# First mixer: convolution taps on VectorE, norms by fours, and the copies of queries and keys issued by GpSimd, head 0's before the value projections

## The chip, the cores and the metric

The kernel runs on one core of a Trainium2 chip. The metric is the device time of one execution in microseconds (us). Several executions are timed, and one more is recorded by the hardware profiler. All times below on a common axis ("at 487 us") count from the start of the span of that profiled execution. Engines are named as the profile names them: PE is TensorE's matmuls, PEld its weight loads, DVE is VectorE, ACT is ScalarE, POOL is GpSimd, SP is SyncE; "POOLq" and "SPq" are DMA issues on those engines' queues.

## The reference, cut to what matters

A sequence of 512 tokens of width 1024 passes through feed-forward blocks and mixers. The change touches one mixer, the first. It has two halves whose outputs are concatenated and projected: a gated delta net (4 heads of 128) and an attention (8 heads of 64) with a bias that depends on the distance of query and key.

```
qkv = silu(short_conv(qkv, conv_w))            # 5 taps along the tokens, per channel
q, k, v = l2_normalize(qkv[0]), l2_normalize(qkv[1]), qkv[2]
...                                            # decay g and beta per token and head
tmat = triangular_solve(eye + lmat, eye)       # chunks of 64 tokens
o    = scan over the chunks, forward and backward
o    = rms_norm(o_fwd + o_bwd, norm_w) * silu(z)
...
logits = q k^T + bias                          # the attention half
out = softmax(logits) v
```

Here l2_normalize divides by the root of the sum of squares over the 128 features of a head; the attention's queries and keys get an RMS norm of their own over 64 features.

## The kernel before, in words

Data in float32 is split into a high and a low part in a reduced format, and each product of two such matrices is three matmuls of TensorE (xh by wh, xh by wl, xl by wh). So each weight block is loaded by a DMA (`raw`, SyncE's queue), cast by ScalarE (`wh`) and subtracted by VectorE (`wl`) before TensorE can use it. The sequence of work on each engine is set by a scheduler from the code's order and the dependences; each engine runs its own queue in order, and buffers come from pools with a tag and a number of slots, which rotate.

The first mixer lasts from about 396 to 870 us. Its parts, in the order of the code:

- **Convolution.** Twelve tiles of 128 channels by 512 tokens (m = 0 to 3 queries, 4 to 7 keys, 8 to 11 values) go through a pipeline of three steps, `conv`, `sums`, `rest`, in which step j of tile m runs beside step 0 of tile m + j. `conv` projects a tile (`pqkv` in PSUM), scales it into a padded tile (`pad`, VectorE), and makes five taps: the first by ScalarE, the other four by VectorE (`cv<-pad,vc,cv`). For m = 8 and 9 the four taps are made by ScalarE into `tap` and added by GpSimd. Then comes a Silu (ScalarE). `sums` squares a query or key tile (`sq`, ScalarE), sums over the features with TensorE (`pss`), and makes the inverse root on VectorE, in `rsqrt`, a chain of 11 small ops with three Newton steps, and in all 14 small ops with the scaling ahead and the split into high and low behind (`rv`, `rt`, `ry`, `yh`, `yl`, 128x4 each). `rest` spreads the result over the features with TensorE (`pn`) and multiplies the tile. For a value tile `rest` turns it (TensorE, `pvt`; copied out by ScalarE, `vt`).
- **Decays.** Per head the products of keys with keys and queries (`pkk`, `pqk`) and the decays (`pgr`, `et`), from which the tiles `B` and `IT` come.
- **Solve.** A triangular solve of 32x32 blocks for all heads on VectorE, 31 steps of two ops (`dX`, `dT`), with a way out to memory and back (`dgi`, `dR`), and then two levels of products per head (`bl` made by GpSimd, `py` by TensorE).
- **Scan.** 32 units (`psc`, `pso`, `vn`); its operands come back from memory by GpSimd's queue (`ld<-ntd`).
- **Norm of O**, four tiles, one by one, each with its own `rsqrt`.
- **Attention.** Projections of queries and keys (`psw`) in pairs of tiles with a norm by pairs (`Ym`, `yxm`, 128x16), written to memory (`qkd`, GpSimd's queue). Value projections (`psv`). Then a pipeline over 8 heads by 4 query tiles: `prepare(h)` brings two copies of a head's keys and of its queries from memory (`T<-qkd`), casts them (ScalarE, `K`, `Q`), and takes the low parts (GpSimd); it also loads the bias (`bq`). `pS` are the scores, `P` the softmax exponentials (ScalarE), `ptp` and `PT` the turn, `po` the product with the values. `prepare(h + 1)` is called at the second query tile of head h, `prepare(0)` at the very first.
- **Gate.** `psz` are projections of the gate z, whose Silu needs another activation table on ScalarE than the exponential (`ACT_TABLE_LOAD`).

The code's order is not the engines' order: the matmuls of `psw`, `psv` and `psz` depend on little and are put between the steps of the convolution, the solve, the scan and the attention. After the attention GpSimd loads four tables for a later mixer (`uqt`) and copies parts of them (`uq`). The buffers of `T` come from the tag `sT` (5 slots), shared with `pad` and the projections' tiles; `sqt` (3 slots) is the tag of the squares.

Of the kernel before, what the change touches and what calls it, by code (L numbers as in the profile page):

```python
# [13 lines left out]
AF = mybir.ActivationFunctionType  # L14
ALU = mybir.AluOpType
# [3 lines left out]
NT = 512  # L19
# [185 lines left out]
class Builder:  # L205
# [424 lines left out]
        return dst  # L630


    def copies(self, src, s, n, tag):
# [6 lines left out]
    def stackK(self, src, s, tags, rows=True):  # L640

        T = self.copies(src, s, 2, tags[0])
# [7 lines left out]
    def stackQ(self, src, s, tags, rows=True):  # L650

        T = self.copies(src, s, 2, tags[0])
# [159 lines left out]
    def mixer1(self):  # L812
        nc = self.nc
        S, S0 = slice(MT, NC), slice(0, NT)
        toks = SEQ
        XH, XL, rs, rsc = self.norm(toks, "mix")
# [56 lines left out]
        def conv(m, _):  # L873
# [17 lines left out]

        def sums(m, cv):
            if m >= 8:
                self.act(cv, cv, AF.Silu)
            return cv, self.row_scales(cv, chunks, 128, 1.0, self.mx) if m < 8 else None

        def rest(m, got):
            cv, y = got
            if m < 8:
                self.row_apply(cv, y, chunks, 128, 128 ** -0.5 if m < 4 else 1.0, self.mx)  # L900
            else:
                pt = self.mx("pvt")
                for c in range(4):
                    self.tr(pt[:, 128 * c:128 * c + 128], cv[:, 128 * c:128 * c + 128])
                vt = self.slab("u", "vt", width=NT)
                self.acopy(vt, pt)
                cv = vt
            C[m] = cv

        staged(12, conv, sums, rest)  # L910
        q, k, vt = C[0:4], C[4:8], C[8:12]


# [169 lines left out]

        staged(32, old, values, update)

        for c in (1, 2, 0, 3):
            ss, sv, sy, sx = (self.small(n, 4, bufs=2) for n in ("nv4", "rv4", "ry4", "rt4"))
            sq = self.slab("u", "sq", width=NT)
            self.act(sq, O[c], AF.Square)
            nc.vector.tensor_reduce(out=ss, in_=by_c(sq), op=ALU.add, axis=mybir.AxisListType.X)  # L1090
            self.ts(sv, ss, 1.0 / 128, ALU.mult, EPS, ALU.add)
            self.rsqrt(sy, sv, sx)
            o3 = by_c(O[c])
            self.mul(o3, o3, sy.unsqueeze(2).to_broadcast([128, 4, 128]))


        sw = self.small("sw", 1)
# [15 lines left out]
        def normed(i, got):  # L1113
# [2 lines left out]
                nc.gpsimd.dma_start(out=qkd[m, :, S], in_=t[:, S])  # L1116

        staged(4, proj, sums, normed)
        V = [self.slab("V", "sV", width=NT) for _ in range(4)]
        staged(4, lambda m, _: self.projV(XH, XL, toks, "psv"), lambda m, t: self.turnV(  # L1120
            t, toks, lambda i, ps: self.act(V[i][:, cc[m]], ps, AF.Copy, scale=rsc[:, i:i + 1]), self.acc))


        Yh, Yl = [None] * 8, [None] * 8
# [2 lines left out]
        def prepare(h):  # L1127
            p, x = divmod(h, 2)
            r = slice(64 * x, 64 * x + 64)
            K = self.stackK(qkd[4 + p, r, :], S, ("sT", "u"), False)  # L1130
            Q = self.stackQ(qkd[p, r, :], S, ("sT", "u"), False)
            heads[h] = {"K": K, "Q": Q, "Y": heads[h - 1]["Y"] if x else self.slab("y", "Y", width=NT),
                        "bq": self.toeplitz(1, h, 0, 0, 896, bpool.tile([128, 1024], F32, tag="bq", name="bq", bufs=2)),
                        **{n: self.small("rs" + n, 4, bufs=2) for n in ("mx", "nm", "den", "rec")}}

        def scores(i, _):
            h, t = divmod(i, 4)
            if i == 0:
                prepare(0)
            if t == 1 and h < 7:  # L1140
                prepare(h + 1)
            u = heads[h]
# [702 lines left out]
```

## Time and profile before

| | us |
|---|---|
| median of 3 runs | 3268.3 (3267.72 to 3269.59) |
| the profiled execution's own time | 3267.1 |
| its span | 3265.3 |
| TensorE busy | 3136.8 |
| VectorE busy | 1747.0 |
| ScalarE busy | 1140.8 |
| GpSimd busy | 511.2 |

The span is the time from the first to the last instruction of the profiled execution; some 1.8 us lie around it. A row of a timeline gives the start, the duration, the engine, the line of the code (often a helper's), the operation, and what it writes and reads by the names above. In brackets stands how long the engine had been idle before it, and who released it.

### The profile page before, as it was taken

The page shows a single profiled execution, that of the slowest core. Times are in us where ns is not written, and L with a number is a line of the kernel's source. Part 1 is how long each engine was busy: PE and PEld are TensorE (multiplying, and loading weights), DVE is VectorE, ACT ScalarE, POOL GpSimd, SP SyncE. Part 2 cuts the span into 40 slices and gives each one's busy share as a digit, 9 for nine tenths or more (in the row PEclk, how much of TensorE's full clock was granted, in tenths as well). Part 3 has the DMA queues.
Part 4 walks back from the last instruction along what each step waited for, and adds up shares of the span by engine and source line. Part 5 has one row for each costly group of instructions (what it writes and reads, how often), then busy time and mean ns, then how long its engine had stood idle before and what let it go on. Part 6 is the DMA issues. An engine that isn't in the chain of part 4 may idle for free. (4 is left out here: it accounts for less than half of the span.)

```text
span 3265.3 us, 47205 instructions
## 1 busy us (share of the span) xinstructions
PE 3136.8 (96%) x18654; PEld 2678.6 (82%) x18654; DVE 1747.0 (54%) x3602; ACT 1140.8 (35%) x1946; POOL 511.2 (16%) x605
## 2 busy tenths in 40 slices
PE   8999989898999999998999999999999899999998
PEld 6778768876788889988887999999878686688886
DVE  4443377653444445764676744433675386754433
ACT  4322253256422233222554332222322364232221
POOL 1000010322000011432123400000351223400000
PEclk9999999898999999998999999999999899999999
DMA  4334313233223324233342523233223343523332
GB/s 132 100 98 132 98 59 97 83 106 94 71 92 96 94 94 125 81 93 106 120 125 86 180 91 91 91 95 119 87 83 116 124 137 100 183 91 96 92 95 79
DMA packets 121270, 337.24 MB, mean 103 GB/s; under 512 B 28853, under 2 KB 29248, under 8 KB 121048
## 3 DMA queue, kind: packets, MB, share of 16 engines
q1 hardware_dynamic: 87656, 267.95, 26.3%
q0 software_dynamic: 21712, 54.51, 5.5%
q10 hardware_dynamic: 11680, 11.76, 1.1%
q8 instruction: 147, 2.41, 0.3%
q14 instruction: 75, 0.61, 0.1%
HBM read 298.42 MB, written 39.56 MB: 104 GB/s over the span
## 5 line engine op out<-in xcount | busy, mean ns | idle before, releaser
L269 ACT CAST wh<-raw 128x1024 fp32r<-128x1024 f32 (+1 forms) x448 | 462.9, 1034 | 1465.8 <-issue 629.6
L247 DVE TENSOR_TENSOR wl<-raw,wh 128x1024 fp32r<-128x1024 f32 (+1 forms) x448 | 556.1, 1242 | 428.2 <-ACT wh L269 427.0
L241 PE MATMUL pg<-xl,wh 128*128 128x512 f32 (+1 forms) x880 | 282.2, 353 | 13.1 <-DVE xl L259 13.1
L241 PE MATMUL pg<-xh,wl 128*128 128x512 f32 (+1 forms) x880 | 280.5, 351 | 0.0
L241 PE MATMUL pg<-xh,wh 128*128 128x512 f32 (+1 forms) x880 | 280.4, 351 | 0.0
L241 PE MATMUL pu<-xl,wh 128*128 128x512 f32 (+1 forms) x880 | 280.2, 351 | 0.0
L241 PE MATMUL pu<-xh,wl 128*128 128x512 f32 (+1 forms) x880 | 280.0, 351 | 0.0
L241 PE MATMUL pd<-hl,wh 128*128 128x512 f32 (+1 forms) x880 | 279.8, 351 | 0.0
L241 PE MATMUL pd<-hh,wl 128*128 128x512 f32 (+1 forms) x880 | 279.3, 350 | 0.0
L241 PE MATMUL pu<-xh,wh 128*128 128x512 f32 (+1 forms) x880 | 279.2, 350 | 0.0
L241 PE MATMUL pd<-hh,wh 128*128 128x512 f32 (+1 forms) x880 | 278.6, 349 | 0.0
L241 PE MATMUL pgz<-xl,wh 128*128 128x264 f32 (+1 forms) x768 | 223.3, 339 | 8.3 <-ACT wh L269 6.8
L247 DVE TENSOR_TENSOR fb<-pu,rs 128x512 f32<-128x512 f32 (+1 forms) x110 | 62.7, 586 | 287.7 <-PE pu L241 287.7
L241 PE MATMUL pgz<-xh,wl 128*128 128x264 f32 (+1 forms) x768 | 214.1, 328 | 1.8 <-DVE wl L247 1.8
L241 PE MATMUL pgz<-xh,wh 128*128 128x264 f32 (+1 forms) x768 | 213.8, 329 | 0.0
L241 PEld LDWEIGHTS pg<-xl,wh 128*128 128x128 f32 x880 | 154.5, 189 | 38.4 <-DVE xl L259 15.2
L241 PEld LDWEIGHTS pu<-xh,wl 128*128 128x128 f32 x880 | 154.4, 189 | 25.1 <-issue 2.6
L241 PEld LDWEIGHTS pg<-xh,wl 128*128 128x128 f32 x880 | 155.0, 189 | 24.1 <-issue 1.7
L241 PEld LDWEIGHTS pg<-xh,wh 128*128 128x128 f32 x880 | 154.5, 189 | 24.4 <-issue 0.9
L241 PEld LDWEIGHTS pu<-xh,wh 128*128 128x128 f32 x880 | 153.9, 188 | 24.0 <-issue 0.9
L241 PEld LDWEIGHTS pd<-hh,wh 128*128 128x128 f32 x880 | 153.8, 188 | 23.5
L241 PEld LDWEIGHTS pd<-hh,wl 128*128 128x128 f32 x880 | 154.0, 188 | 22.6
(496 smaller groups left out, 6343.8 us busy)
## 6 DMA issues: line engine op xcount, KB each, us to landing
raw<-in_win SPq DMA_DIRECT2D x136, 512.0 KB
raw<-in_gu SPq DMA_DIRECT2D x88, 512.0 KB
raw<-in_f1gu SPq DMA_DIRECT2D x44, 512.0 KB
raw<-in_f2gu SPq DMA_DIRECT2D x44, 512.0 KB
raw<-in_dn SPq DMA_DIRECT2D x32, 512.0 KB
raw<-in_wout SPq DMA_DIRECT2D x24, 512.0 KB
gates<-g POOLq DMA_DIRECT2D x32, 264.0 KB, 2.8
gr<-gates SPq DMA_DIRECT2D x32, 264.0 KB
```

Source lines behind the costliest of these rows:

```text
L241: return self.nc.tensor.matmul(out=out, lhsT=lhsT, rhs=rhs, start=start, stop=stop)
L247: return (eng or self.nc.vector).tensor_tensor(out=out, in0=a, in1=b, op=op)
L269: return self.nc.scalar.copy(out=out, in_=in_)
```

## The change

- `conv`: for all tiles the taps two to five are made by VectorE, and the Silu follows in `conv`; `tap` and GpSimd's additions are gone.
- `sums` of the convolution: the four query tiles get one chain of small ops together (`group_scales`, on 128x16, in `Ym` and `yxm`), at m = 3, and the four key tiles at m = 7, instead of one chain on 128x4 per tile. They are multiplied in the third step, now `scaled`, two tiles each at m = 4, 5, 8 and 9.
- Norm of O: by twos, one chain on 128x8 for two tiles.
- `prepare(h)`: both copies `T<-qkd` are issued by GpSimd instead of SyncE, into the tag `sqt`; `prepare(0)` is called ahead of the value projections.

```diff
+    def copies(self, src, s, n, tag, eng=None):
...
-        self.nc.sync.dma_start(out=t[:n * rows, s], in_=src[:, s].unsqueeze(0).to_broadcast([n, rows, w]))
+        (eng or self.nc.sync).dma_start(out=t[:n * rows, s], in_=src[:, s].unsqueeze(0).to_broadcast([n, rows, w]))
...
             for i in range(1, 5):
-                if m not in (8, 9):
-                    self.stt(cv, pad[:, i:i + 512], self.v("conv", 5 * m + i), cv, ALU.mult, ALU.add)
-                else:
-                    t = self.slab("u", "tap", width=NT)
-                    self.act(t, pad[:, i:i + 512], AF.Copy, scale=self.v("conv", 5 * m + i))
-                    self.add(cv, cv, t, nc.gpsimd)
-            if m < 8:
-                self.act(cv, cv, AF.Silu)
+                self.stt(cv, pad[:, i:i + 512], self.v("conv", 5 * m + i), cv, ALU.mult, ALU.add)
+            self.act(cv, cv, AF.Silu)
             return cv
...
         def sums(m, cv):
+
+            C[m] = cv
+            if m in (3, 7):
+                ys.update(zip(range(m - 3, m + 1), self.group_scales(C[m - 3:m + 1], chunks, 128, 1.0, self.mx)))
+
+        def scaled(m, _):
+            for i in {4: (0, 1), 5: (2, 3), 8: (4, 5), 9: (6, 7)}.get(m, ()):
+                self.row_apply(C[i], ys[i], chunks, 128, 128 ** -0.5 if i < 4 else 1.0, self.mx)
             if m >= 8:
...
-        for c in (1, 2, 0, 3):
-            ss, sv, sy, sx = (self.small(n, 4, bufs=2) for n in ("nv4", "rv4", "ry4", "rt4"))
...
+        for two in ((1, 2), (0, 3)):
+            ss, sv, sy, sx = (self.small(n, 8, bufs=2) for n in ("nv8", "rv8", "ry8", "rt8"))
...
+            K = self.stackK(qkd[4 + p, r, :], S, ("sqt", "u"), False, nc.gpsimd)
+            Q = self.stackQ(qkd[p, r, :], S, ("sqt", "u"), False, nc.gpsimd)
...
+        prepare(0)
         V = [self.slab("V", "sV", width=NT) for _ in range(4)]
```

The instructions move on several engines, which the diff alone doesn't show. On VectorE, in the convolution, at the norms of the last key tiles, the order before has two chains of small ops interleaved (`rt_3145` and `rt_3223` are those of two tiles):

```order
L259 SCALAR_TENSOR_TENSOR rt_3145<-rt_3145,rv_3144 128x4
L263 TENSOR_SCALAR rv_3222<-pss 128x4
L259 SCALAR_TENSOR_TENSOR ry_3146<-rt_3145,ry_3146 128x4
L263 TENSOR_SCALAR rt_3223<-rv_3222 128x4
L247 TENSOR_TENSOR rt_3145<-ry_3146 128x4
L263 TENSOR_SCALAR ry_3224<-rt_3223 128x4
```

The order after, at the end of the chain of the four key tiles:

```order
L259 SCALAR_TENSOR_TENSOR Ym<-Ym 128x16 x2
L247 TENSOR_TENSOR wl<-raw,wh 128x1024
L272 CAST yxm<-Ym 128x16
L259 SCALAR_TENSOR_TENSOR cv<-pad,vc,cv 128x512
L247 TENSOR_TENSOR yxm<-Ym,yxm 128x16
L259 SCALAR_TENSOR_TENSOR cv<-pad,vc,cv 128x512 x3
L259 SCALAR_TENSOR_TENSOR cv<-cv,pn 128x512 x2
```

One chain for four tiles has taken the place of four; its end stands among the taps of a value tile, ahead of the multiplication of the key tiles (`cv<-cv,pn`). On GpSimd, at the start of the attention, behind the last loads of the scan, the order before is this (`K` and `Q` are the low parts; the numbers tell the heads apart, 5513 and 5518 are head 0's):

```order
L1044 DMA ld<-itd 128x512
L247 TENSOR_TENSOR K_5513<-T,K_5512 64x512
L247 TENSOR_TENSOR Q_5518<-T,Q_5518 64x512
L247 TENSOR_TENSOR K_5538<-T,K_5537 64x512
L247 TENSOR_TENSOR Q_5543<-T,Q_5543 64x512
L629 DMA bq<-bper_575 128x1x896
```

The order after (5167 and 5172 are head 0's):

```order
L1037 DMA ld<-itd 128x512
L629 DMA uqt<-bper_584 128x1x416
L247 TENSOR_TENSOR K_5167<-T,K_5166 64x512
L629 DMA uqt<-bper_584 128x1x416
L247 TENSOR_TENSOR Q_5172<-T,Q_5172 64x512
L637 DMA T<-qkd 128x1x512 x2
L1207 COPY uq<-uqt 128x64
L1209 COPY uq<-uqt 128x16
```

The loads `uqt` of the later mixer, which stood behind head 5 before, stand here by twos; the copies `uq` of the first two come next, and the key part of head 1 behind them, and the copies `T` of later heads stand between the parts; both copies of head 0 and the key copy of head 1 are not among these rows, since they are issued some 30 instructions earlier, beside the masks `bl`. On ScalarE, in the middle of the attention, the order before has other work between a gate's Silu and the second of its two table loads:

```order
L266 ACT_TABLE_LOAD
L266 ACTIVATE z<-z 128x512
L269 COPY yt<-ptr 128x512
L266 ACTIVATE Y<-po,rsrec 128x64
L269 CAST Yh<-yt 128x512
L269 COPY PT<-ptp 128x512
L266 ACT_TABLE_LOAD
L266 ACTIVATE P,rsden<-P,rsnm 128x512
```

In the order after it is like this there, and at each of the four gates:

```order
L269 CAST wh<-raw 128x1024
L269 COPY PT<-ptp 128x512
L266 ACTIVATE Y<-po,rsrec 128x64
L266 ACT_TABLE_LOAD
L266 ACTIVATE z<-z 128x512
L266 ACT_TABLE_LOAD
L266 ACTIVATE P,rsden<-P,rsnm 128x512 x2
```

The two loads of a pair have only the Silu between them now; before, this was so at two gates of four.

## Rows read from the trace of the kernel before

**Rows 1.** The page, busy time of TensorE: us, share of the span, instructions.

```profile
PE 3136.8 (96%) x18654; PEld 2678.6 (82%) x18654; DVE 1747.0 (54%) x3602; ACT 1140.8 (35%) x1946; POOL 511.2 (16%) x605
```

**Rows 2.** Timeline of TensorE in the convolution, and its first py.

```profile
480.74 0.40 PE L241 MATMUL pqkv<-xh,wh 128*128 128x512 f32 x1
487.37 0.45 PE L241 MATMUL pn<-idr,yl 128*128 128x128 f32 x1 [6.23 <-DVE rt L247]
...
507.83 0.39 PE L241 MATMUL psw<-xl,wh 128*128 128x512 f32 x1
508.06 0.40 PE L241 MATMUL psw<-xh,wl 128*128 128x512 f32 x1
...
508.90 0.39 PE L241 MATMUL pkk<-cv 128*128 128x128 f32 x2
...
604.02 1.13 PE L241 MATMUL py<-n,bl 128*128 128x128 f32 x8 [0.96 <-DVE n L247]
```

**Rows 3.** Windows: length, busy us by engine, granted clock, DMA share, GB/s.

```profile
490.00:500.00 10.00, 10.00 (x50) 8.66 (x50) 7.14 (x36) 0.63 (x1) 0.00 (x0) 0.78 0.18 52
720.00:730.00 10.00, 9.57 (x39) 7.73 (x39) 2.95 (x11) 7.16 (x14) 0.60 (x2) 0.67 0.28 87
780.00:790.00 10.00, 10.00 (x39) 8.06 (x38) 2.27 (x6) 5.84 (x13) 3.07 (x7) 0.50 0.43 129
790.00:800.00 10.00, 9.73 (x51) 7.69 (x49) 3.97 (x14) 4.58 (x11) 2.70 (x5) 0.76 0.38 102
800.00:810.00 10.00, 5.98 (x18) 4.06 (x19) 2.80 (x8) 3.02 (x8) 2.49 (x5) 0.58 0.17 51
```

**Rows 4.** Timeline of TensorE in the attention, the ends of three holes.

```profile
720.43 1.11 PE L244 MATMUL ptp<-ct,P 128*128 128x128 f32 x4 [4.02 <-ACT P L266]
...
779.41 0.48 PE L244 MATMUL ptp<-ct,P 128*128 128x128 f32 x1 [3.35 <-ACT PT L269]
...
804.02 1.51 PE L241 MATMUL pS<-K,Q 128*128 128x512 f32 x2 [4.29 <-POOL Q L247]
```

**Rows 5.** Timeline of VectorE: small ops of two norms, one whole chain's ends, the solve.

```profile
477.81 0.17 DVE L263 TENSOR_SCALAR ry<-rt 128x4 int32<-128x4 int32 x1
...
485.92 1.23 DVE L259 SCALAR_TENSOR_TENSOR ry<-rt,ry 128x4 f32<-128x4 f32 x1
...
548.29 0.17 DVE L263 TENSOR_SCALAR Ym<-pss 128x16 f32<-128x16 f32 x1 [0.99 <-PE pss L241]
...
551.02 0.18 DVE L247 TENSOR_TENSOR yxm<-Ym,yxm 128x16 fp32r<-128x16 f32 x1
...
552.25 0.20 DVE L247 TENSOR_TENSOR dX<-dM,dT 128x31 f32<-128x31 f32 x1
```

**Rows 6.** Timeline of GpSimd in the convolution and in the attention.

```profile
476.47 10.66 POOL L247 TENSOR_TENSOR cv<-cv,tap 128x512 f32<-128x512 f32 x8 [6.64 <-ACT tap L266]
...
802.25 0.24 POOL L1212 COPY uq<-uqt 128x64 f32<-128x64 f32 x1 [5.72 <-DMA uqt<-bper]
```

**Rows 7.** Groups of VectorE, 396 to 500 us: busy us, mean ns, idle before.

```profile
L259 DVE SCALAR_TENSOR_TENSOR cv<-pad,vc,cv 128x512 f32<-128x512 f32 x36 | 26.2, 746 | 0.0
L259 DVE SCALAR_TENSOR_TENSOR ry<-rt,ry 128x4 f32<-128x4 f32 x24 | 7.9, 331 | 0.1
L247 DVE TENSOR_TENSOR rt<-ry 128x4 f32<-128x4 f32 x24 | 4.7, 198 | 0.1
```

**Rows 8.** Timeline of ScalarE in the attention.

```profile
712.83 0.62 ACT L269 CAST K<-T 128x512 fp32r<-128x512 f32 x1 [5.88 <-DMA T<-qkd]
...
718.10 0.62 ACT L269 CAST Q<-T 128x512 fp32r<-128x512 f32 x1 [3.94 <-DMA T<-qkd]
...
774.13 1.28 ACT L266 ACT_TABLE_LOAD   x1
```

**Rows 9.** Timeline of SyncE's DMA queue at the attention's start.

```profile
704.30 28.24 SPq L637 DMA_DIRECT2D T<-qkd  x7
```

**Rows 10.** DMA issues, 680 to 800 us: queue, count, KB, median us to landing.

```profile
ld<-ntd POOLq DMA_DIRECT2D x2, 256.0 KB, 3.4
```

More of the change, by code (lines that the diff above doesn't have):

```diff
@@ L630, in toeplitz, with stackK @@
         return dst
-    def copies(self, src, s, n, tag):
+    def copies(self, src, s, n, tag, eng=None):
         t = self.slab(tag, "T")
         rows, w = src.shape[0], s.stop - s.start
-        self.nc.sync.dma_start(out=t[:n * rows, s], in_=src[:, s].unsqueeze(0).to_broadcast([n, rows, w]))
+        (eng or self.nc.sync).dma_start(out=t[:n * rows, s], in_=src[:, s].unsqueeze(0).to_broadcast([n, rows, w]))
         return t
-    def stackK(self, src, s, tags, rows=True):
-        T = self.copies(src, s, 2, tags[0])
+    def stackK(self, src, s, tags, rows=True, eng=None):
+        T = self.copies(src, s, 2, tags[0], eng)
         K1, K2 = self.slab(tags[1], "K1", F32R), self.slab(tags[1], "K2", F32R)
@@ L648, in stackK, with stackQ @@
         return K1, K2
-    def stackQ(self, src, s, tags, rows=True):
-        T = self.copies(src, s, 2, tags[0])
+    def stackQ(self, src, s, tags, rows=True, eng=None):
+        T = self.copies(src, s, 2, tags[0], eng)
         Q1 = self.slab(tags[1], "Q1", F32R)
@@ L881, in conv @@
             for i in range(1, 5):
-                if m not in (8, 9):
-                    self.stt(cv, pad[:, i:i + 512], self.v("conv", 5 * m + i), cv, ALU.mult, ALU.add)
-                else:
-                    t = self.slab("u", "tap", width=NT)
-                    self.act(t, pad[:, i:i + 512], AF.Copy, scale=self.v("conv", 5 * m + i))
-                    self.add(cv, cv, t, nc.gpsimd)
-            if m < 8:
-                self.act(cv, cv, AF.Silu)
+                self.stt(cv, pad[:, i:i + 512], self.v("conv", 5 * m + i), cv, ALU.mult, ALU.add)
+            self.act(cv, cv, AF.Silu)
             return cv
         def sums(m, cv):
-            if m >= 8:
[L894 to L901, printed above, removed]
+            C[m] = cv
[4 more added lines that the diff above has]
+                self.row_apply(C[i], ys[i], chunks, 128, 128 ** -0.5 if i < 4 else 1.0, self.mx)
+            if m >= 8:
                 pt = self.mx("pvt")
                 for c in range(4):
[L904 to L910, printed above, removed]
+                    self.tr(pt[:, 128 * c:128 * c + 128], C[m][:, 128 * c:128 * c + 128])
+                C[m] = self.slab("u", "vt", width=NT)
+                self.acopy(C[m], pt)
+        ys = {}
+        staged(12, conv, sums, scaled)
         q, k, vt = C[0:4], C[4:8], C[8:12]
@@ L1084, in mixer1 @@
         staged(32, old, values, update)
-        for c in (1, 2, 0, 3):
-            ss, sv, sy, sx = (self.small(n, 4, bufs=2) for n in ("nv4", "rv4", "ry4", "rt4"))
-            sq = self.slab("u", "sq", width=NT)
-            self.act(sq, O[c], AF.Square)
-            nc.vector.tensor_reduce(out=ss, in_=by_c(sq), op=ALU.add, axis=mybir.AxisListType.X)
+        for two in ((1, 2), (0, 3)):
+            ss, sv, sy, sx = (self.small(n, 8, bufs=2) for n in ("nv8", "rv8", "ry8", "rt8"))
+            for i, c in enumerate(two):
+                sq = self.slab("u", "sq", width=NT)
+                self.act(sq, O[c], AF.Square)
+                nc.vector.tensor_reduce(out=ss[:, 4 * i:4 * i + 4], in_=by_c(sq), op=ALU.add, axis=mybir.AxisListType.X)
             self.ts(sv, ss, 1.0 / 128, ALU.mult, EPS, ALU.add)
             self.rsqrt(sy, sv, sx)
-            o3 = by_c(O[c])
-            self.mul(o3, o3, sy.unsqueeze(2).to_broadcast([128, 4, 128]))
+            for i, c in enumerate(two):
+                o3 = by_c(O[c])
+                self.mul(o3, o3, sy[:, 4 * i:4 * i + 4].unsqueeze(2).to_broadcast([128, 4, 128]))
         sw = self.small("sw", 1)
@@ L1134, in prepare @@
                         **{n: self.small("rs" + n, 4, bufs=2) for n in ("mx", "nm", "den", "rec")}}
+        prepare(0)
+        V = [self.slab("V", "sV", width=NT) for _ in range(4)]
+        staged(4, lambda m, _: self.projV(XH, XL, toks, "psv"), lambda m, t: self.turnV(
+            t, toks, lambda i, ps: self.act(V[i][:, cc[m]], ps, AF.Copy, scale=rsc[:, i:i + 1]), self.acc))
         def scores(i, _):
             h, t = divmod(i, 4)
-            if i == 0:
-                prepare(0)
             if t == 1 and h < 7:
```

5 lines of the change are left out of this document (removed).

## Prediction

> **What bounds the kernel now.** I read the page first: over the span TensorE is busy 96 per cent [rows 1], so the only thing an edit of other engines can give is TensorE time that was idle or slow. The first mixer runs from about 396 to 870 us of the span. Its idle and slow places come from the timeline of TensorE and the windows of 10 us. Two places matter. The first is the convolution stage: TensorE's rows stand 6.23 us apart there, and the releaser named is a VectorE op on a small tile [rows 2]. Behind the hole the granted clock is 0.78 of full in the mean of one window [rows 3], that is, part of it at 1.2 instead of 2.4 GHz. The second is the attention, where TensorE waits 4.02, 3.35 and 4.29 us, for ScalarE twice and for GpSimd once [rows 4], each followed by windows at 0.67, 0.50 and 0.58 [rows 3].
>
> Why VectorE is late in the first place is seen in its own timeline: a small op on 128x4 takes 0.17 us at 477.81 and 1.23 us at 485.92 [rows 5]. In between GpSimd runs its eight additions of taps, 10.66 us in one go [rows 6], about the length of one of them per stretched op. TensorE waits for the chain of such ops that makes the norms of the last key tiles.
>
> **The change, part by part.**
>
> *Taps and norms.* Removed: eight GpSimd additions and eight ScalarE taps, and with the additions the thing that stretches the small ops. Added on VectorE: 8 taps of 0.746 us [rows 7], 6.0 us. Removed on VectorE: eight chains of 14 small ops; two of their forms alone make 7.9 + 4.7 = 12.6 us [rows 7]. Added in their place: two chains on 128x16; one such chain stands in the attention's projections already and takes from 548.29 to 551.2, 2.9 us [rows 5], so 5.8 for two. VectorE, which is the full engine here, gets 12.6 - 5.8 - 6.0 = 0.8 us lighter by these forms alone, so not heavier. The hole, 6.2 us, and the slow clock behind it go. What the clock cost: between 487.4 and 494.4 TensorE runs ops at about half rate; the 490 to 500 window, busy throughout at 0.78, lost 2.2 us, and the norm matmuls ahead of it, from 487.37 to 490, another 1.3 (2.6 us at half the rate). Together 6.2 + 2.2 + 1.3 = 9.7 us.
>
> What is next late: the last value tile. After its scaling by VectorE it needs four taps (0.67 us apart), the weight split queued between them and ScalarE's Silu before TensorE can turn it. I walked the new order with the durations of these rows and get the matmuls of the key products (pkk) at 497.5 instead of 508.90 [rows 2], with 12 fewer matmuls of the attention's projections ahead of them. These 12 come later, at 0.233 us each (the pitch from 507.83 to 508.06 [rows 2]), 2.8 us. The term is 508.9 - 497.5 - 2.8 = **-8.6 us**, so a new wait of about 1.1 us is in it. Bounds: -9.7 with no new wait; -4.2 if the new wait is 2 us and the clock falls behind it as it did here (3.5).
>
> *The solve.* In the kernel before, the first step of the triangular solve (dX) stands on VectorE at 552.25, behind the norm chain that begins at 548.29 [rows 5]; in the new order it stands ahead of it. The walk gives the end of the solve some 13 us earlier and the first product behind it (py, at 604.02 [rows 2]) at 595.4 with 10 more value-projection matmuls done, 2.3 us. That is 604.0 - 595.4 + 2.3 = 10.9 in all, **-2.3 us** beyond the first term. Bounds: 0, if TensorE's queue of projections is what sets it, to -4. In this stage GpSimd's queue gets the first copy of keys ahead of two masks (bl); the copy waits for the landing of the key tile in memory. In the walk the masks are still ready some 4 us ahead of TensorE; without that cover the term falls to 0.
>
> *The norms of O by twos.* Two chains of small ops instead of four, on VectorE while TensorE runs the gate's projections. I cost it at nothing; if that cover fails, it is a gain of up to 1 us, since only work is taken away.
>
> *Copies of queries and keys by GpSimd.* Before, ScalarE's queue stands twice on a copy still in flight: 5.88 us in front of the first key cast of head 1, 3.94 in front of its query cast, and the softmax exponentials of head 0 stand behind both [rows 8]. SyncE's queue needs 28.24 us for seven such copies [rows 9], 4.0 each. In the new order both copies of head 0 and the key copy of head 1 stand ahead of the value projections, 100 us early, so these waits have no cause left; only the query copy of head 1 is still issued at the start. Of the trace's operations the nearest to it is a 256 KB load by GpSimd's queue: 3.4 us to landing [rows 10], about when ScalarE reaches the cast. So the 4.02 us hole and its clock (a third of the 720 window's 9.6 busy us, 3.2) go: **-7.2 us**. The other two holes I leave as they are. Bounds: all three holes with their clock go (4.0 + 3.2, 3.35 + 7.3, 4.3 + 2.5 = 24.7 us; from the windows of [rows 3], busy time times the missing clock), or none does and one new hole of 3.35 + 4 us comes.
>
> The Trainium skill, page "DMA: Bandwidth & Descriptors", section "Issuing engines are not separate DMA queues", says that copies from any engine's queue run on the same 16 DMA engines and that another issuer saves only the issuing time. By it the later heads' copies land no earlier than before, and only what is issued earlier in the program gains; by the row of 3.4 us they would land 0.6 us sooner. The term above takes nothing from that difference, so both give the same sum; they differ on the first rival.
>
> **Sum.** -8.6 - 2.3 - 7.2 = -18.1. The profiled run took 3267.1 us (span 3265.3 and 1.8 around it), 1.2 below the median of the runs, so 3267.1 - 18.1 = 3249.0 there and **3250.2 us** for the median.
>
> **The rivals.**
>
> *All holes of the attention go* (-8.6 - 2.3 - 24.7 = -35.6, 3232.7 us). For it: the third hole, at 804.02, ends with GpSimd's query part, which stood behind a copy waiting 5.72 us for a table load [rows 6, 4]; that load and copy move to the attention's first heads. Against: the load's wait is still on GpSimd's queue, now ahead of head 1's key part, and ScalarE's table loads remain.
>
> *The attention gives nothing* (-10.9, 3257.4 us). For it: the exponentials of head 0 come earlier, but behind them stands the pair of activation table loads, 1.28 us each [rows 8], as before, and GpSimd's queue waits for table loads earlier than before.
>
> *Table loads pace the attention: slower.* ScalarE loads another activation table for each gate tile (z) and loads back; with nothing between but the gate's own Silu, as from 774.13 on, that is 2.6 us and the Silu in which no exponential runs [rows 8], and the hole of 3.35 us at 779.41 [rows 4] stands behind one such pair. Before, two of the four gates have the two loads this close; in the new order all four do. If each cost what the one at 774 did (3.35 + 7.3 = 10.7 us) and three new holes come, then -18.1 + 32 = +14, 3282 us. It turns slower than before from the second new hole on (-18.1 + 21.4 = +3.3, 3271.5 us). Against: the first close pair, right behind the hole that ends at 720.43, has no hole behind it.
>
> *The change doesn't do what it says:* small ops stretch beside something else than GpSimd's additions. Then the hole stays with less in it; the time is that of the second rival plus some 5 us, 3262.
>
> **How the numbers follow.** Forecast 3250 (3243 to 3257): 0.45. All holes gone, 3233 (3228 to 3243): 0.15. Attention gives nothing, 3257 (3255 to 3262): 0.18. One or two new holes, or the stretch stays (3262 to 3275): 0.13. Three new holes (above 3275): 0.09. A measurement here tells a difference of 0.2 per cent, 6.5 us, from none. Faster by more: 0.45 + 0.15 + 0.17 = 0.77; within: 0.14; slower: 0.09. The range leaves out the lower half of the first rival (0.07) and what lies above 3266 (0.13): 3234 to 3266.
>
> **What the new profile would show.** Right: no row of TensorE in the convolution stage with an idle of over 2.5 us, small VectorE ops there at 0.15 to 0.2 us, the windows from 480 to 500 at full clock; the first py at about 595; in the attention no wait of ScalarE for the first heads' copies, and no hole ahead of the second exponential of head 0. Wrong: a hole ahead of the turn of the last value tile, with slow windows behind it; holes released by ScalarE's exponentials behind each table load; GpSimd's query or key parts as releaser in heads 1 and 2, behind a wait for a table load.

## The result, and the profile after

The kernel after takes 3251.48 us (median of 4 runs, 3241.55 to 3254.03) against 3268.09 (4 runs, 3267.72 to 3269.59): a ratio of 0.9937, with a 95 per cent interval of 0.9922 to 0.9952. The forecast of 3250.2 is 1.3 us off. The sum was right, but two of its terms were not.

The page of after, with the span, the busy times that answer to [rows 1], and the DMA packets (before there were 28853 under 512 B, of 121270):

```profile
span 3252.2 us, 47046 instructions
PE 3137.4 (96%) x18654; PEld 2679.8 (82%) x18654; DVE 1745.9 (54%) x3502; ACT 1136.4 (35%) x1938; POOL 514.9 (16%) x613
DMA packets 127635, 337.27 MB, mean 104 GB/s; under 512 B 36245, under 2 KB 36640, under 8 KB 127416
```

TensorE is as busy as before, so the 13.1 us that its span is shorter are idle time that went. TensorE's timeline of after in the convolution, which answers to [rows 2]; the columns are as there:

```profile
472.85 3.68 PE L241 MATMUL pn<-idr,yxm 128*128 128x128 f32 x32
476.37 4.02 PE L241 MATMUL pss<-ones,sq 128*128 128x1 f32 x24
...
480.82 0.63 PE L241 MATMUL pqkv<-xh,wh 128*128 128x512 f32 x1
481.25 0.63 PE L241 MATMUL pqkv<-xl,wh 128*128 128x512 f32 x1
...
488.00 0.39 PE L241 MATMUL pqkv<-xl,wh 128*128 128x512 f32 x1
488.23 0.40 PE L241 MATMUL pqkv<-xh,wl 128*128 128x512 f32 x1
...
504.46 0.67 PE L244 MATMUL pvt<-ct,cv 128*128 128x128 f32 x4 [1.84 <-ACT cv L266]
504.95 0.60 PE L241 MATMUL pkk<-cv 128*128 128x128 f32 x2
...
604.79 1.95 PE L241 MATMUL py<-n,bl 128*128 128x128 f32 x16
```

The 6.23-us hole is gone, and a wait of 1.84 us ahead of the last value tile has come, as forecast. Not forecast is the stretch from 480.82: 128x512 matmuls stand 0.43 us apart there and 0.23 at 488, so TensorE runs at 1.2 instead of 2.4 GHz, with no idle time in front. Ahead of it stand 32 spreading matmuls (`pn`) and 24 sums that write one column each (`pss`). The windows, as in [rows 3], in the convolution:

```profile
470.00:480.00 10.00, 10.00 (x68) 9.42 (x68) 10.00 (x19) 4.79 (x7) 0.13 (x2) 0.88 0.34 103
480.00:490.00 10.00, 10.00 (x33) 8.34 (x34) 5.19 (x16) 1.66 (x3) 0.00 (x0) 0.60 0.00 0
490.00:500.00 10.00, 10.00 (x68) 8.85 (x67) 8.24 (x16) 4.40 (x7) 0.00 (x0) 1.00 0.16 52
```

Busy time times the missing clock is what a window lost: 10.00 × (1 - 0.88) = 1.2 and 10.00 × (1 - 0.60) = 4.0, together 5.2 us. In the attention, TensorE's rows that answer to [rows 4], and ScalarE's that answer to [rows 8]:

```profile
715.40 0.66 PE L244 MATMUL ptp<-ct,P 128*128 128x128 f32 x4 [0.86 <-ACT P L266]
...
774.21 0.77 PE L244 MATMUL ptp<-ct,P 128*128 128x128 f32 x4 [2.56 <-ACT P L266]
```
```profile
714.01 0.62 ACT L269 CAST Q<-T 128x512 fp32r<-128x512 f32 x1 [5.67 <-DMA T<-qkd]
...
770.11 1.28 ACT L266 ACT_TABLE_LOAD   x1
772.05 1.28 ACT L266 ACT_TABLE_LOAD   x1
```

Two of the three holes are gone. The one that is left, behind a pair of table loads, is 2.56 us instead of 3.35. ScalarE still waits 5.67 us for the query copy of head 1, but TensorE has other work then and stands for only 0.86.

To compare stages over all kernels, two numbers are read from each trace: the sum of TensorE's idle stretches of over 0.3 us, and the sum over the 10-us windows of busy time times missing clock. In us, idle + clock, for the convolution (380 to 545), the solve and the scan (545 to 700), and the attention (700 to 880); the last columns are the profiled execution's own time and the ratio of the medians to the kernel before:

| kernel | 380–545 | 545–700 | 700–880 | all | its time | ratio |
|---|---|---|---|---|---|---|
| before | 11.7 + 3.3 | 10.3 + 11.5 | 16.4 + 14.7 | 67.9 | 3267.1 | 1 |
| after | 7.2 + 9.5 | 10.2 + 10.6 | 6.7 + 10.5 | 54.7 | 3254.0 | 0.9937 |
| after_again | 7.2 + 9.6 | 9.9 + 8.1 | 3.5 + 6.8 | 45.1 | 3247.6 | 0.9935 |
| conv_alone | 7.5 + 11.6 | 9.3 + 10.8 | 17.4 + 16.2 | 72.8 | 3270.8 | 1.0000 |
| taps_alone | 6.0 + 4.7 | 11.6 + 8.1 | 9.3 + 12.5 | 52.2 | 3251.8 | 0.9942 |
| copies_alone | 10.2 + 6.7 | 12.0 + 9.3 | 8.2 + 11.3 | 57.7 | 3255.5 | 0.9962 |
| spread_norms | 9.4 + 4.8 | 10.1 + 10.7 | 4.9 + 9.5 | 49.4 | 3253.4 | 0.9936 |
| half_bunch | 6.1 + 8.6 | 9.5 + 8.0 | 7.3 + 17.8 | 57.3 | 3252.8 | 0.9943 |
| pairs_copies | 9.5 + 1.7 | 10.7 + 9.0 | 4.9 + 11.4 | 47.2 | 3248.1 | 0.9929 |
| issuer_sync | 7.5 + 9.8 | 8.9 + 7.2 | 9.0 + 7.3 | 49.7 | 3259.0 | 0.9937 |
| late_prepare | 7.2 + 8.0 | 10.2 + 9.0 | 6.0 + 11.1 | 51.5 | 3249.0 | 0.9926 |
| taps_copies | 6.0 + 1.3 | 8.9 + 8.4 | 7.4 + 9.5 | 41.5 | 3240.6 | 0.9912 |
| taps_copies_o | 6.0 + 1.4 | 8.9 + 10.5 | 8.8 + 1.3 | 36.9 | 3240.7 | 0.9924 |
| q_own_slots | 6.0 + 0.0 | 10.1 + 6.6 | 5.5 + 8.0 | 36.2 | 3236.2 | 0.9911 |

The time less the column "all" is 3196 to 3204 in every row but issuer_sync's (3209), so the three stages account for the differences between the other kernels to within 8 us. Before to after is -13.2 by the table and -13.1 by the two times. A single profile scatters: after_again is the same kernel as after. A hole counts whole in the stage in which it begins. The one ahead of the attention's first turn of a value tile (1.51 us before, 2.03 after) begins at 701.6 before and at 699.0 after, and in after_again the hole ahead of its first scores (0.87) begins below 700 too. So 2 to 3 us of the difference between the last two stages are the place of the border.

### The profile page after: what moved, and what is told of

Same layout as the page of the kernel before. It is cut to its first block, busy times and chain, and to the rows that moved or that the text cites. A ratio compares the mean times of both kernels' runs of the same rounds, so it can differ in the third digit from the quotient of the medians.

```text
span 3252.2 us, 47046 instructions
## 1 busy us (share of the span) xinstructions
PE 3137.4 (96%) x18654; PEld 2679.8 (82%) x18654; DVE 1745.9 (54%) x3502; ACT 1136.4 (35%) x1938; POOL 514.9 (16%) x613
## 2 busy tenths in 40 slices
DMA packets 127635, 337.27 MB, mean 104 GB/s; under 512 B 36245, under 2 KB 36640, under 8 KB 127416
```

## The experiments

The kernels of a paragraph were run beside the kernel before on the same chip; `before` had medians of 3269.1, 3273.1 and 3269.8 us in the three sets, so ratios are compared, or times within a set. "Copies" below means the change's last part whole: issued by GpSimd, into `sqt`, head 0's ahead of the value projections.

### One part alone: taps_alone, conv_alone, copies_alone, spread_norms

**taps_alone**: the kernel before with all taps on VectorE; norms tile by tile, copies on SyncE.

```diff
-                if m not in (8, 9):
-                    self.stt(cv, pad[:, i:i + 512], self.v("conv", 5 * m + i), cv, ALU.mult, ALU.add)
-                else:
...
+                self.stt(cv, pad[:, i:i + 512], self.v("conv", 5 * m + i), cv, ALU.mult, ALU.add)
+            self.act(cv, cv, AF.Silu)
```

> The kernel before with the first part of the change alone: all taps on VectorE, norms still one by one, copies still by SyncE. Both theories: GpSimd's additions are gone, so the eight stretched small ops (1.1 to 1.2 us each) fall to 0.2 us, 8 us of VectorE, against 8 taps at 0.67 us, 5.4 us. The hole of 6.2 us in the convolution shrinks to about 3.5 us. Theory A (the clock, not VectorE, is what the convolution stage of the changed kernel pays with): no long bunch of narrow norm matmuls here, so the clock falls at most behind the hole; 3268 - 3 to - 6, about 3263 us. Theory B (the convolution's terms were sized rightly, and one profiled execution was unlucky): the same, 3263 us. If small ops are still stretched to over 1 us, the cause named for the hole is wrong.

Measured: 3251.75 us (3247.18 to 3256.18), ratio 0.9942 [0.9929, 0.9954]. This one edit has nearly all of the change's gain, 17.4 us where both theories had 3 to 6, and a far smaller hole than their 3.5 us. A small VectorE op, TensorE at the norm that stood behind the hole, and the windows where after is slow:

```profile
485.14 0.16 DVE L259 SCALAR_TENSOR_TENSOR ry<-rt,ry 128x4 f32<-128x4 f32 x1
```
```profile
499.32 0.30 PE L241 MATMUL pn<-idr,yl 128*128 128x128 f32 x1 [0.58 <-DVE yl L247]
```
```profile
470.00:480.00 10.00, 10.00 (x53) 8.23 (x51) 9.85 (x30) 4.47 (x8) 0.13 (x2) 1.00 0.35 105
480.00:490.00 10.00, 10.00 (x55) 8.28 (x54) 9.84 (x39) 4.16 (x6) 0.00 (x0) 1.00 0.17 54
```

The hole of 6.23 us has become one of 0.58, and the clock stays at full behind it. The attention, which this edit does not touch, lost 21.8 us instead of 31.1. What differs there is SyncE's DMA queue; first before, which answers to [rows 9], then taps_alone:

```profile
686.84 1.27 SPq L637 DMA_DIRECT2D T<-qkd  x2
703.84 0.34 SPq L321 DMA_DIRECT2D raw<-in_wout  x1
```
```profile
680.98 0.34 SPq L321 DMA_DIRECT2D raw<-in_wout  x1
681.50 23.08 SPq L637 DMA_DIRECT2D T<-qkd  x6
```

Before, seven copies stand behind a weight load that is issued at 703.84. In taps_alone that load is issued at 680.98, and the six copies behind it start 23 us earlier than before; ScalarE waits for none of them. So 9.3 of the 15.7 us that the table gives to this edit come from the scheduler's new order in a stage that the edit leaves alone, and 4.3 from the convolution. That the place of the weight load is the reason is read from these rows; no run moved it alone.

**conv_alone**: the kernel before with the whole convolution of after, taps and norms by fours; copies on SyncE.

> The kernel before with taps on VectorE and norms by fours, nothing else. Theory A: the hole is gone, but TensorE runs at half clock behind 32 norm matmuls and some 24 sums in one row, and waits 1.8 us for the last value tile: 0 to -4 us, about 3266 us, the slow stretch (about 9 us long) in its profile. Theory B: -8.6 - 2.3 = -11 us, 3257 us, windows at full clock from 470 to 500.

Measured: 3270.78 us (11 runs, 3264.76 to 3273.23), ratio 1.0000 [0.9991, 1.0009]. The difference to taps_alone is the norms by fours, and they undo all that the taps gain: 20.6 us by the table, 8.4 of them in the convolution and 11.8 in the attention. In the convolution two stretches run slow, the 10 us from 450 and the 10 us from 480; at the start of the attention ScalarE waits for copies again, which stand behind a weight load issued at 705.44:

```profile
450.00:460.00 10.00, 10.00 (x30) 8.17 (x29) 5.14 (x8) 3.52 (x5) 0.26 (x4) 0.54 0.18 57
...
480.00:490.00 10.00, 10.00 (x34) 8.75 (x35) 7.03 (x18) 1.59 (x3) 0.00 (x0) 0.50 0.02 7
```
```profile
711.63 0.62 ACT L269 CAST Q<-T 128x512 fp32r<-128x512 f32 x1 [4.00 <-DMA T<-qkd]
...
723.31 0.62 ACT L269 CAST Q<-T 128x512 fp32r<-128x512 f32 x1 [5.19 <-DMA T<-qkd]
```

**copies_alone**: the kernel before with the copies; taps and norms as before.

```diff
-            K = self.stackK(qkd[4 + p, r, :], S, ("sT", "u"), False)
-            Q = self.stackQ(qkd[p, r, :], S, ("sT", "u"), False)
+            K = self.stackK(qkd[4 + p, r, :], S, ("sqt", "u"), False, nc.gpsimd)
+            Q = self.stackQ(qkd[p, r, :], S, ("sqt", "u"), False, nc.gpsimd)
...
+        prepare(0)
         V = [self.slab("V", "sV", width=NT) for _ in range(4)]
```

> The kernel before with the copies of queries and keys issued by GpSimd into the other tag, and head 0 prepared ahead of the value projections, nothing else. Theory A: the attention gives 9 to 13 us, about 3257 us, all three holes of 3.4 to 4.3 us gone or down to one of 2.5. Theory B: only the hole of head 0 goes, -7 us, 3261 us.

Measured: 3257.56 us (3255.46 to 3264.63), ratio 0.9962 [0.9950, 0.9975]; the attention lost 19.5 us instead of 31.1. GpSimd's additions are still there, and so are the stretched small ops and the hole:

```profile
482.18 1.20 DVE L259 SCALAR_TENSOR_TENSOR ry<-rt,ry 128x4 f32<-128x4 f32 x1
```
```profile
487.64 0.45 PE L241 MATMUL pn<-idr,yl 128*128 128x128 f32 x1 [4.67 <-DVE rt L247]
```

With taps_alone this shows the cause of the hole from both sides: this op takes 1.20 us where GpSimd adds and 0.16 where it doesn't. Not every small op beside an addition is stretched. In the kernel before, within the 10.66 us of the additions, seven take 0.66 to 1.24 us, one 0.38, and the others 0.15 to 0.17; the op of 0.17 us at 477.81 [rows 5] lies inside that stretch, not ahead of it. The last stretched op ends where the last addition does (485.92 + 1.23 = 487.15, 476.47 + 10.66 = 487.13). The Trainium skill, page "SBUF — State Buffer", section "SBUF: two separate sides", says that VectorE and GpSimd share one pair of ports under an exclusive lock, which an op of VectorE needs if it has two inputs in SBUF or runs in a two-port mode, and that the loser blocks for the other's whole instruction; the stretched op with its two inputs agrees, at 1.20 us beside additions of 1.33 (10.66 / 8).

**spread_norms**: after, with each tile squared and summed at its own step into a shared tile of PSUM, still one chain of small ops for four tiles; the multiplication is one tile per step.

```diff
-            if m in (3, 7):
-                ys.update(zip(range(m - 3, m + 1), self.group_scales(C[m - 3:m + 1], chunks, 128, 1.0, self.mx)))
...
+                for i, (c, k) in enumerate(chunks):
+                    self.mm(ps[:, 4 * a + i:4 * a + i + 1], sq[:, c:c + k], self.ones[:, 0:1])
+                if a == 3:
...
-            for i in {4: (0, 1), 5: (2, 3), 8: (4, 5), 9: (6, 7)}.get(m, ()):
+            for i in {4: (0,), 5: (1,), 6: (2,), 7: (3,), 8: (4,), 9: (5,), 10: (6,), 11: (7,)}.get(m, ()):
```

> The changed kernel with one thing altered: the sums over features of each query or key tile are made as the tile is done, into one shared PSUM tile, so that 16 of the 24 narrow sums leave the bunch in front of the last value tiles; still one chain of small ops for four tiles; the 32 spreading matmuls stay together. Theory A (the bunch of narrow matmuls is what TensorE's clock falls behind): the half-clock stretch of about 9 us is gone or much shorter, -4 us against the changed kernel, 3247 us. Theory B (the fall of the clock has nothing to do with the bunch): as the changed kernel, 3251 us, with the slow stretch in the same place.

Measured: 3248.30 us (3247.25 to 3254.76), ratio 0.9936 [0.9924, 0.9948].

```profile
470.00:480.00 10.00, 8.80 (x56) 8.35 (x56) 8.45 (x16) 3.91 (x6) 0.00 (x0) 0.82 0.18 54
480.00:490.00 10.00, 10.00 (x44) 8.00 (x44) 7.84 (x22) 3.53 (x5) 0.00 (x0) 0.84 0.02 5
```
```profile
476.10 1.71 PE L241 MATMUL pss<-ones,sq 128*128 128x1 f32 x8 [1.20 <-ACT sq L266]
```

The sums are in a row of 8 here instead of 24. The clock's loss in these windows is 1.6 + 1.6 = 3.2 us instead of 5.2, with 1.2 us of idle time more: smaller, not gone. The slow stretch begins right behind that new hole, with the eight sums at 476.10 (1.71 us here, 0.95 at full clock), so this run doesn't tell what a shorter row of sums does by itself. By time it can't be told from after.

### After against its own parts: after_again, taps_copies, issuer_sync, late_prepare

**after_again** is the kernel after, once more, beside the three below.

> The changed kernel itself, with a second profile. Its first profile has three half-clock stretches in the convolution: 437.7 to 443.4 us, behind a hole of 3.08 us that the kernel before has as well, with no slow clock behind it; 478.8 to 487.7, behind the bunch of norm matmuls; and 505 to 507, behind a wait of 1.84. Theory A (the bunch pulls the clock down each time, the stretch behind the 3.08 us hole is chance): the stretch at 479 is there again, that at 438 may be gone; median 3251 us. Rival R (all of it is chance): the stretch at 479 is gone or elsewhere in this profile, and single runs of one kernel lie 5 to 10 us apart.

Measured: 3251.51 us (6 runs, 3247.64 to 3255.00), ratio 0.9935 [0.9923, 0.9948]. The slow stretch of the convolution is there again:

```profile
480.00:490.00 10.00, 10.00 (x36) 8.26 (x35) 5.31 (x17) 2.77 (x4) 0.00 (x0) 0.67 0.00 0
```

**taps_copies**: taps_alone with the copies, that is, after without the norms by fours and by twos.

> The changed kernel without its norms by fours and by twos: taps on VectorE, copies by GpSimd with head 0 ahead of the value projections, norms one by one. Theory A (norms by fours bring nothing, since the bunch costs what the chains saved): idle and slow TensorE time as with the taps alone up to the attention, 28 us, and as with the copies in it, 18 us; 68 us before, so -20 to -22, 3247 us. Rival N (with the copies on GpSimd the norms by fours are needed): 3255 us or more, with a new hole at the key norms of over 2 us. Rival S (taps and copies repair the same thing in the attention, and the taps nothing else): as with the taps alone, 3252 us.

Measured: 3244.15 us (4 runs, 3240.59 to 3245.25), ratio 0.9912 [0.9898, 0.9925]. No run of it is as long as the shortest of after_again: the norms by fours and by twos cost 3251.51 - 3244.15 = 7.4 us. Its convolution lost 7.3 us instead of 16.8:

```profile
470.00:480.00 10.00, 10.00 (x57) 8.38 (x55) 9.85 (x31) 5.21 (x8) 0.00 (x0) 1.00 0.27 102
480.00:490.00 10.00, 10.00 (x57) 8.40 (x56) 9.83 (x37) 3.40 (x5) 0.00 (x0) 1.00 0.18 53
```

**issuer_sync**: after, the copies issued by SyncE; the tag and head 0's place are as after.

```diff
-            K = self.stackK(qkd[4 + p, r, :], S, ("sqt", "u"), False, nc.gpsimd)
-            Q = self.stackQ(qkd[p, r, :], S, ("sqt", "u"), False, nc.gpsimd)
+            K = self.stackK(qkd[4 + p, r, :], S, ("sqt", "u"), False)
+            Q = self.stackQ(qkd[p, r, :], S, ("sqt", "u"), False)
```

> The changed kernel with the copies of queries and keys issued by SyncE again; their buffers (three slots of the squares' tag) and the place of head 0's in the code stay as changed. In the order the first five copies stand ahead of the output weights' loads on SyncE's queue. Theory A (what held the copies was the weight load ahead of them on SyncE's queue, not SyncE's way to issue): about the time of the changed kernel, 3251 us within 4, and no wait of ScalarE of over 4 us for the copies of head 0. Rival P (GpSimd's queue brings them faster): 7 us lost, 3258 us or more, with holes in head 0 and 1.

Measured: 3252.73 us (3247.71 to 3258.97), ratio 0.9937 [0.9923, 0.9951], the same as after. SyncE's DMA queue has the first copies ahead of that weight load now:

```profile
594.92 2.60 SPq L637 DMA_DIRECT2D T<-qkd  x3
...
697.09 1.89 SPq L637 DMA_DIRECT2D T<-qkd  x2
...
702.65 0.83 SPq L321 DMA_DIRECT2D raw<-in_wout  x1
```

So the issuer isn't what gains. What is left of the edit is the earlier place in the queue, ahead of the weight load, and the tag with its slots; these runs don't part the two. The rule that the prediction weighed (the Trainium skill, page "DMA: Bandwidth & Descriptors", section "Issuing engines are not separate DMA queues") agrees with this pair of runs.

**late_prepare**: after, with `prepare(0)` back at its old place in `scores`.

```diff
-        prepare(0)
         V = [self.slab("V", "sV", width=NT) for _ in range(4)]
...
             h, t = divmod(i, 4)
+            if i == 0:
+                prepare(0)
```

> The changed kernel with head 0's preparation called at the start of the attention again, not ahead of the value projections. In the order the scheduler still puts the first three copies ahead of the scan's loads on GpSimd's queue. Theory A: the place in the code hardly matters once the copies are on GpSimd's queue: 3251 us within 4. Rival E (the early call brings the gain): 3258 us, with holes in head 0.

Measured: 3246.93 us (3242.64 to 3261.11), ratio 0.9926 [0.9909, 0.9944]: no difference to after that can be told. On GpSimd the first copies are issued some 100 us ahead of the attention all the same, since the scheduler moves them there:

```profile
604.50 0.83 POOL L637 DMA_DIRECT2D T<-qkd  x1 [1.45 <-ACT ys L269]
```

### What in the norms costs, and what can be had: half_bunch, pairs_copies, taps_copies_o, q_own_slots

**half_bunch**: after, but only the high part of the norms is spread; their low part `yl` isn't in the product, and there are half as many `pn`.

```diff
-                self.row_apply(C[i], ys[i], chunks, 128, 128 ** -0.5 if i < 4 else 1.0, self.mx)
+                ph = self.mx("pn")
+                for j, (c0, k0) in enumerate(chunks):
+                    self.mm(ph[:, c0:c0 + k0], ys[i][0][:k0, j:j + 1].to_broadcast([k0, 128]), self.idr[:k0, :k0])
+                self.stt(C[i][:, 0:512], C[i][:, 0:512], 128 ** -0.5 if i < 4 else 1.0, ph, ALU.mult, ALU.mult)
```

> The changed kernel with half of the spreading matmuls in the convolution left out: only the high part of the norms is spread, so 16 instead of 32 of them stand ahead of the 12 to 16 narrow sums (the low part of the queries' and keys' norms is missing in the result). Theory A (the clock falls behind the length of the bunch): the bunch is 3.5 to 4 us instead of 7; the slow stretch at 470 to 490 us, 5.1 us lost in both profiles of the changed kernel, falls to 2 us or less; with 16 + 16 matmuls of 0.11 us fewer, 3.6 us, the time is 3251 - 7 = 3244 us. Rival R (the fall has nothing to do with the bunch's length): 5 us lost as before, -3.6 us alone, 3248 us.

Measured: 3252.04 us (4 runs, 3251.13 to 3252.95), ratio 0.9943 [0.9930, 0.9956]. The row of `pn` is 16 long instead of 32, that of sums 24 as in after, and the loss behind them is the same, 1.8 + 3.4 = 5.2 us:

```profile
472.85 1.90 PE L241 MATMUL pn<-idr,yxm 128*128 128x128 f32 x16
474.61 3.59 PE L241 MATMUL pss<-ones,sq 128*128 128x1 f32 x24
```
```profile
470.00:480.00 10.00, 10.00 (x58) 9.01 (x58) 8.81 (x18) 4.08 (x6) 0.13 (x2) 0.82 0.32 105
480.00:490.00 10.00, 10.00 (x35) 8.21 (x34) 4.82 (x12) 2.15 (x3) 0.00 (x0) 0.66 0.01 2
```

So halving the spreading matmuls left the loss as it was. Neither theory's time came: this profile loses 7.9 us more in the attention than that of after.

**pairs_copies**: taps_copies with the norms by twos, the multiplication one tile per step.

```diff
+            if m in (1, 3, 5, 7):
+                ys.update(zip(range(m - 1, m + 1), self.group_scales(C[m - 1:m + 1], chunks, 128, 1.0, self.mx)))
...
+            for i in {2: (0,), 3: (1,), 4: (2,), 5: (3,), 6: (4,), 7: (5,), 8: (6,), 9: (7,)}.get(m, ()):
```

> Taps on VectorE, copies by GpSimd, O's norms one by one, and the norms of the convolution by pairs of tiles: in the order 16 spreading matmuls and 4 to 8 sums stand together, half of the bunch of the fours, twice that of the norms one by one. Theory A: the clock loss between 450 and 500 us lies between 0 (one by one) and 5.1 us (fours), about 2; 3246 us, or 3244 if the saved small ops (four chains of 14) help VectorE. Rival N (the fours' loss comes from the late multiplication of the last tiles, not from the bunch): full clock there, and 3243 us or less.

Measured: 3247.01 us (3243.96 to 3253.59), ratio 0.9929 [0.9916, 0.9942]. The convolution lost 9.5 + 1.7 us. By time it lies between taps_copies and after, with an interval that overlaps both.

**taps_copies_o**: taps_copies with the norm of O by twos, as in the change's diff.

> Taps on VectorE, copies by GpSimd, the convolution's norms one by one, O's norms by twos: the changed kernel without the norms by fours alone. Theory A: O's norms by twos are worth nothing that can be measured, so as with taps and copies, 3244 us within 4. Rival O (they are what makes the changed kernel 7 us slower than taps and copies, by their place at the attention's start): 3250 us or more.

Measured: 3242.33 us (3240.19 to 3258.88), ratio 0.9924 [0.9906, 0.9943], not to be told from taps_copies. The norm of O is worth nothing that these runs can show.

**q_own_slots**: taps_copies, the query copies in their old tag `sT`.

```diff
-            Q = self.stackQ(qkd[p, r, :], S, ("sqt", "u"), False, nc.gpsimd)
+            Q = self.stackQ(qkd[p, r, :], S, ("sT", "u"), False, nc.gpsimd)
```

> Taps and copies with the query copies in the other tag's five slots, so that the query copies of the first heads needn't wait for slots of the key copies. In the changed kernel ScalarE waits 5.67 us for head 1's query copy, in taps and copies 3.63. Theory A: this wait goes, and the holes of head 0 with it (1.45 us and the clock at 700, 1.6): -2 to -3 us against taps and copies, 3241 to 3242 us. Rival Q (the wait lies beside other work): no difference, 3244 us.

Measured: 3240.72 us (3236.18 to 3245.52), ratio 0.9911 [0.9897, 0.9926]. ScalarE waits for no copy any more, yet the ratio is that of taps_copies; TensorE has a new hole where GpSimd makes a query part late:

```profile
748.62 1.52 PE L241 MATMUL pS<-K,Q 128*128 128x512 f32 x2 [3.26 <-POOL Q L247]
```

Every kernel here but conv_alone beats the kernel before, by intervals that leave out 1, and taps_copies beats after in the set that had both.

## Why the prediction was right, point by point

The bound was right, and so were the hole's cause and the late copies at the attention's start. That the sum came within 1.3 us is luck: a convolution term that was too good by 7 to 10 us and an attention term that was too small by 5 to 14 made up for each other.

**The bound, the hole and its cause: right.** The time moved with TensorE's idle and slow time alone, and taking GpSimd's additions away took the hole away (taps_alone; in copies_alone, where they stay, it is there). The rival that the small ops stretch beside something else is out.

**Taps and norms, -8.6 us: wrong, about +1.7.** By the table the convolution lost 16.7 us after and 15.0 before. By the term's own milestone, the first `pkk` at 504.95 instead of 497.5 with 12 fewer projections ahead of it as forecast, 508.90 - 504.95 - 2.8 = 1.1 us were gained. The hole went (idle 11.7 to 7.2), and the new wait was 1.84 us, inside the bound of 2, with 1.4 us of slow clock behind it (500 to 510 us, 8.16 busy at 0.83). The step that failed is the one that costs the norms by fours at VectorE's time alone (5.8 us for two chains instead of 12.6). The same edit puts 24 one-column sums and 32 spreading matmuls in one row on TensorE, and the text had no word on them. Behind the row TensorE runs at 1.2 GHz until shortly before 488, with nothing idle in front: 5.2 us here, 3.4 to 5.2 in the five other kernels with the row of 24 sums, and none between 470 and 490 us in taps_alone, taps_copies, taps_copies_o and q_own_slots, where the norms go one by one. Another 2.9 us are the clock behind the hole that ends at 437.70, on which the last section has more. The forecast's bounds, -9.7 to -4.2, did not hold it: they reckoned with a slow clock only behind the new wait.

**The solve, -2.3 us: of the right size, but not told from scatter.** The stage lost 20.8 us instead of 21.8 (18.0 in after_again), -1.0 to -3.8, or -3.0 to -6.7 with the holes around 700 us counted alike. Its milestone was wrong all the same: the first py stands at 604.79, not 595.4, with 10 value projections more done ahead of it. At 0.233 us each that is a gain of 2.3 - 0.8 = 1.5 us by that point, where the first two terms together had 10.9.

**The norm of O, 0: right** as far as taps_copies_o can tell.

**The attention, -7.2 us: right in kind, too small.** It lost 17.2 us instead of 31.1, or 10.3 in after_again: -13.9 to -20.8, or -11.9 to -17.9 with the holes around 700 us counted alike. The first hole went as forecast. The third went too, which the text left in the sum and put into the first rival; GpSimd's load and copy of the tables stand earlier, and nothing waits there any more. The hole behind the table loads stayed, at 2.56 us. The rival in which table loads pace the attention did not come: there are four close pairs, and one hole.

**The landing of a copy** was taken to be 3.4 us, by the nearest row of GpSimd's queue [rows 10]. It was 9.1, which the DMA view of 695 to 800 us shows (queue, count, KB, median us to landing):

```profile
T<-qkd POOLq DMA_DIRECT2D x13, 256.0 KB, 9.1
```

GpSimd issued head 1's query copy at 704.66, so with 3.4 us it would have landed at 708.1, when ScalarE was ready for it; ScalarE waited until 714.01. It cost little, since TensorE had the gate's projections to do. In q_own_slots, where five copies are issued by 676, the wait is gone.

**Do the parts add?** Alone, the taps give a ratio of 0.9942 and the copies 0.9962, whose product is 0.9904; together they give 0.9912, with 0.9904 inside its interval. So by time they add as far as these runs can tell. In the attention they overlap: each alone takes the hole of 4.02 us away (none is left in taps_alone, 1.43 us in copies_alone), and by the table 9.3 and 11.6 us alone become 14.2 together. A profile's scatter there, 6.9 us between after and after_again, is too large to settle it.

**The signs that the text named.** Right was that the small VectorE ops of the convolution's norms take 0.17 us each. Four others of the first list failed: the window from 480 is at 0.60 of the full clock, the first py comes at 604.79, ScalarE still waits 5.67 us, and an idle stretch of over 2.5 us is left, the one of 3.09 us ahead of 437.70, which the kernel before has too and the text overlooked. Of the signs of being wrong one came, the hole ahead of the turn of the last value tile with a slow window behind it. So the mechanism behind the convolution's term was wrong, though the time lay where it was forecast.

**What stays open.** What in the norms by fours slows the clock isn't settled. Halving the spreading matmuls changed nothing (half_bunch). Cutting the row of sums from 24 to 8, with the multiplications one by one, left 3.2 of 5.2 us, behind a new hole of 1.20 (spread_norms). Chains by twos left 1.7 in the whole stage (pairs_copies). No run cut the sums alone.

## What to carry to other kernels

Grouping small work to save one engine instructions also groups what it asks of the others: count the matmuls that come to stand in a row, and look at the granted clock behind a like row before taking the edit as free. Where one engine's small ops are several times longer in one place than in another, look for what the neighbour engine runs beside them; here, moving that work back to the full engine took the hole away, though more than half of what that edit gained came from a queue's new order elsewhere. So compare an edit's gain stage by stage before putting it down to the edit. Price a transfer by its place in the queue, not by the engine that issues it.

## What the runs showed of the hardware that was not expected

**The same hole does not always cost the same clock.** Up to the hole of 3.1 us that ends near 437 us all 14 kernels issue the same 1788 matmuls to TensorE:

```profile
437.70 0.77 PE L241 MATMUL pqkv<-xl,wh 128*128 128x512 f32 x1 [3.09 <-DVE pad L247]
438.69 0.63 PE L241 MATMUL pqkv<-xh,wh 128*128 128x512 f32 x1
```

That is after, whose clock fell to 1.2 GHz; the windows behind the hole are, first for after and then for q_own_slots:

```profile
430.00:440.00 10.00, 6.91 (x26) 5.23 (x25) 5.50 (x7) 4.15 (x6) 0.00 (x0) 0.84 0.35 104
440.00:450.00 10.00, 10.00 (x41) 8.06 (x39) 9.29 (x15) 5.29 (x9) 0.39 (x6) 0.82 0.05 8
```
```profile
430.00:440.00 10.00, 6.91 (x31) 5.30 (x30) 5.40 (x7) 4.17 (x6) 0.00 (x0) 1.00 0.35 102
440.00:450.00 10.00, 9.97 (x52) 8.12 (x51) 10.00 (x21) 6.13 (x10) 0.39 (x6) 1.00 0.12 27
```

After lost 1.1 + 1.8 = 2.9 us there, q_own_slots and before nothing, after_again 1.5; in all, the clock fell right behind this hole in seven of the 14 profiles. In three others, all with norms by fours (conv_alone, issuer_sync, half_bunch), it fell some 12 us later, behind two rows of eight sums with two projections between them and an idle stretch of under 0.4 us ahead: 3.0 to 4.6 us lost from 450 to 460. After has the same rows of sums there, without the idle stretch, and stayed at full clock. Runs of one kernel differ by 2 to 19 us, and part of that may be this.

**Full TensorE, half clock.** The windows from 480 in after and conv_alone are busy for all 10 us, behind a window that is busy for all 10 us too, and the clock is at 0.60 and 0.50. Busy means here that matmuls follow each other without an idle stretch in the profile, the narrow ones included. Idle time is thus not the only thing to look for ahead of a slow stretch.

**A copy by GpSimd's queue** landed in 9.1 us where a load of the same 256 KB on that queue took 3.4 [rows 10]. The packets under 512 B rose by 36245 - 28853 = 7392 with the change; that they are the reason is a guess that no run tested. The copy differs from the load in one more way: it reads 64 rows twice, by a broadcast, into 128 partitions.
